# Seven block products in place of eight for half of the second MLP weight, with weight sums made by adding DMAs

## The chip, the cores and the metric

One Trainium2 chip, one of its cores. The metric is the device time of one execution in microseconds; less is better. Before the change it was 2324.06 us (median of three runs, 2323.91 to 2324.21).

## What is computed

Two layers over 256 tokens of width 2048, all in float32. Each layer is a mixer (a gated linear recurrence in layer 0, gated linear attention in layer 1) and then a dense squared-ReLU MLP; each of the four has a norm ahead of it and behind it and is added to the residual. The change concerns the MLP alone:

```python
def sqrelu_mlp(h, w_up, w_down):
    u = jax.nn.relu(h @ w_up)      # (256, 2048) @ (2048, 8192)
    return (u * u) @ w_down        # (256, 8192) @ (8192, 2048)

for i in range(DEPTH):
    ...
    f = sqrelu_mlp(rmsnorm(h, norm_mlp_pre[i]), mlp_w_up[i], mlp_w_down[i])
    h = h + rmsnorm(f, norm_mlp_post[i])
```

## The kernel before

Every matrix product runs on TensorE with both factors split in two parts: `hi`, the value rounded to the short form that TensorE multiplies in one pass, and `lo`, the rest. One product is then three matmuls, x_hi·w_hi, x_hi·w_lo and x_lo·w_hi (lines 122 to 127). A weight is read from HBM in chunks of 1 MB (`load_chunk`, line 96, always on SyncE's queue, three buffers `raw`), each of two halves of 128x1024. ScalarE makes `hi` of a half (line 102) and VectorE makes `lo` (line 106); five buffers of each are there, so at most five halves are split ahead of TensorE.

The MLP (`mlp`, line 475) goes through the 8192 hidden features in eight groups of 1024 (`GK` = 8 tiles of 128). `up(g)` computes one group of hidden features, transposed, eight times `gemmT` (16 matmuls of 512 columns with `hi`, 16 of 256 columns with `lo`), folds the two halves of the result, applies the squared ReLU and leaves the hi and lo parts in `uT[g]`. `down(g)` multiplies that group by its 1024 rows of `w_dn`: for each of four blocks of 512 output columns (`n`) it reads two chunks and runs `gemm` for both blocks of 128 tokens (`t`), 48 matmuls in all, then adds the two results onto the sums `m[n, t]` on VectorE (line 517). The order is up(0), up(1), down(0), up(2), down(1) and so on; the last block of columns of the last group is handed to `transition` or `final`, which finish the norm and start the next stage.

The code gives the order of the calls; the order in which each engine then gets its instructions is made by a scheduler that simulates the program, except inside blocks that fix it by hand (the start of the program and `transition`). Each engine and each queue works through its own instructions in that order. `Next` takes the first weight halves of the stage that follows ahead of time, into tiles that are free by then.

Of the kernel before, what the change touches and what calls it, by code (L numbers as in the profile page):

```python
# [18 lines left out]
P = 128  # L19
# [11 lines left out]
def trunk(  # L31
# [13 lines left out]
    halfp = ctx.enter_context(tc.tile_pool(name="half", bufs=6))  # L45
    featp = ctx.enter_context(tc.tile_pool(name="feat", bufs=1))
    accp = ctx.enter_context(tc.tile_pool(name="acc", bufs=1))
    small = ctx.enter_context(tc.tile_pool(name="small", bufs=4))
    psmm = ctx.enter_context(tc.tile_pool(name="psmm", bufs=4, space=PSUM))
    pssc = ctx.enter_context(tc.tile_pool(name="pssc", bufs=2, space=PSUM))  # L50
# [87 lines left out]
    def gemmT(wap, idx, X, pool=psmm, tag="mm"):  # L138


        ps = pool.tile([P, 2, T], F32, tag=tag, name=nm("mmT"))
        halves = split_chunk(wap, idx)
        for k in range(KT):
            hi = halves[k // 8][0][:, k % 8 * P:(k % 8 + 1) * P]
            PE.matmul(ps, hi, X.both(k), start=(k == 0), stop=False)  # L145
        for k in range(KT):
            lo = halves[k // 8][1][:, k % 8 * P:(k % 8 + 1) * P]
            PE.matmul(ps[:, 0, :], lo, X.both(k)[:, 0, :], start=False, stop=(k == KT - 1))  # L148
        return ps

    def fold(ps, rr=None):

        u = half()
        A.copy(u, ps[:, 1, :])  # L154
        V.tensor_tensor(u, ps[:, 0, :], u, ALU.add)  # L155
# [141 lines left out]
    def rrow(rs):  # L297
        ps = pstr.tile([P, NT, P], F32, tag="tr", name=nm("psr"))
        for t in range(NT):
            PE.matmul(ps[:, t, :], bc(rs[t], [P, P]), ident, start=True, stop=True)  # L300
        rr = small.tile([P, T], F32, tag="rr", bufs=1, name=nm("rr"))
        A.copy(rr, ps.rearrange("p a b -> p (a b)"))
        return rr

    class Post:
# [13 lines left out]
        def take(self, ps, n, t):  # L319
            self.square(ps, n, t)  # L320
            self.weigh(ps, n, t)
# [19 lines left out]
    class Next:  # L341

        def __init__(self, w, base):
            self.w, self.base, self.raws, self.parts, self.room = w, base, [], [], self.rooms()

        def rooms(self):
            def take(pool, tag, shape):
                return pool.tile(shape, F32R, tag=tag, name=nm(f"s{tag}"))  # L350

            qk = take(featp, "qk", [P, 2, 1024])
# [3 lines left out]
            b = take(big, "big", [P, 4, 1024])  # L356
            for j in range(2):
                yield b[:, 2 * j, :], b[:, 2 * j + 1, :]
            while True:
                yield None  # L360

# [112 lines left out]

    def mlp(layer, w_up, w_dn, X, rs, ps0, then=None):
        GK = 8
        NG = FF // (GK * P)
        uT = [None] * NG
        m = {}
        post = Post(2 + layer)  # L480

        rr = []

        def up(g):
            U = Xhl(GK)
            uT[g] = U
            for b in range(0, GK, 4):
                if g == 0 and b == 0:
                    for t in range(NT):
                        s = tok()  # L490
                        A.activation(s, ps0[t], AF.Relu, scale=rs[t])
                        A.activation(s, s, AF.Square)
                        put_split(transpose4(lambda j: s[:, j * P:(j + 1) * P]), U, 0, t)
                    rr.append(rrow(rs))
                    continue
                for j in range(b, b + 4):
                    u = fold(gemmT(w_up, g * GK + j, X))
                    V.scalar_tensor_tensor(u, u, 0.0, rr[0], ALU.max, ALU.mult)  # L498
                    hi, lo = U.both(j)[:, 0, :], U.both(j)[:, 1, :]
                    A.activation(hi, u, AF.Square)  # L500
                    A.activation(u, u, AF.Square)  # L501
                    V.tensor_tensor(lo, u, hi.bitcast(F32), ALU.subtract)  # L502

        ahead = Next(*then[1:]) if then is not None else None
        plan = {(NG - 2, 2): 2, (NG - 1, 0): 1, (NG - 1, 1): 1, (NG - 1, 2): 1}

        def down(g):
            for n in range(4 if g < NG - 1 else 3):
                ps = gemm(w_dn, n * 16 + 2 * g, GK, uT[g])
                if ahead is not None:  # L510
                    ahead.split(plan.get((g, n), 0))
                for t in range(NT):
                    if g == 0:
                        m[n, t] = tok()
                        V.tensor_copy(m[n, t], ps[t])
                        continue
                    V.tensor_tensor(m[n, t], m[n, t], ps[t], ALU.add)  # L517
                    if g == NG - 1:
                        post.take(m[n, t], n, t)

        up(0)
        for g in range(1, NG):
            up(g)
            down(g - 1)
        post.wp(3)
        down(NG - 1)
        args = (w_dn, 3 * 16 + 2 * (NG - 1), GK, uT[NG - 1], post, {t: m[3, t] for t in range(NT)})
        if then is not None:
            return transition(*args, then[0], ahead)
        final(*args)  # L530
# [412 lines left out]
```

## Time and profile before

| | |
|---|---|
| median of the runs | 2324.06 us |
| the profiled execution | 2323.86 us |
| its span, first to last instruction | 2322.1 us |
| TensorE busy | 2306.9 us, 99% |
| VectorE busy | 1505.1 us, 65% |
| ScalarE busy | 1217.5 us, 52% |
| bytes moved by DMA | 433.61 MB, 187 GB/s in the mean |

In the profile a line such as "PE ... L125" is a matmul that line 125 of the kernel issued; PEld is the load of its stationary operand, DVE is VectorE, ACT is ScalarE, POOL is GpSimd and SP is SyncE, which only issues DMAs here. Matmuls overlap in the pipeline, so what one costs is read from the distance between starts and not from its own duration.

### The profile page before, as it was taken

What the parts mean: (1) busy time and instruction counts of PE and PEld (TensorE: products, weight loads), DVE (VectorE), ACT (ScalarE), POOL (GpSimd) and SP (SyncE); (2) the same over time, 40 slices, a digit from 0 to 9 for tenths busy, and PEclk for the clock granted to TensorE, in tenths of its full rate; (3) what the DMA queues carried; (4) which work ended last, traced back from release to release, by engine and by line L of the source; (5) the groups of instructions that cost most, each with busy time, mean ns of one, the idle gap of its engine ahead of it and who ended that gap; (6) DMA issues with size and microseconds to landing.
All of it is one profiled execution on the core that took longest, in us unless ns stands there. A gap on an engine that the chain in (4) does not pass through costs nothing.

```text
span 2322.1 us, 29521 instructions
## 1 busy us (share of the span) xinstructions
PE 2306.9 (99%) x11720; PEld 1963.4 (85%) x11720; DVE 1505.1 (65%) x2111; ACT 1217.5 (52%) x1755; POOL 0.2 (0%) x4
## 2 busy tenths in 40 slices
PE   9999999999999999999999999999999999999998
PEld 7888888888888888888888888888888888888887
DVE  6887877656565565565676767566656556556556
ACT  7555554556454454454557456554645445445443
POOL 0000000000000000000000000000000000000000
PEclk9999999999999999999999999999999999999999
DMA  8544445545555555555654544454455555555553
GB/s 324 178 167 163 167 163 180 197 166 183 202 187 193 194 188 190 192 196 184 220 177 154 202 157 160 164 214 183 166 197 191 194 194 187 191 191 197 182 199 136
DMA packets 66155, 433.61 MB, mean 187 GB/s; under 512 B 8000, under 2 KB 8384, under 8 KB 15712
## 3 DMA queue, kind: packets, MB, share of 16 engines
q1 hardware_dynamic: 65872, 431.45, 53.8%
q8 instruction: 92, 1.51, 0.3%
q14 instruction: 47, 0.39, 0.0%
q10 hardware_dynamic: 144, 0.26, 0.0%
HBM read 429.59 MB, written 2.10 MB: 186 GB/s over the span
## 4 chain that ended last, share of the span: by engine, by line
PE 97%; DVE 2%; ACT 1%; issue 0%; DMA 0%; SPq 0%; DVEq 0%; ACTq 0%
PE mmT L145 27%; PE mm L127 18%; PE mm L126 18%; PE mm L125 18%; PE mmT L148 14%; PE sc L587 2%; DVE lo L106 1%; PE tr L181 1%; DVE xhl L194 0%; PE sd L622 0%; PE po L671 0%; PE po L674 0%; PE po L673 0%; ACT xhl L192 0%; DMA raw<-w_hin 0%
## 5 line engine op out<-in xcount | busy, mean ns | idle before, releaser
L106 DVE TENSOR_TENSOR lo<-raw,hi 128x1024 fp32r<-128x1024 f32 x779 | 939.2, 1223 | 523.1 <-ACT hi L102 394.2
L102 ACT ACTIVATE hi<-raw 128x1024 fp32r<-128x1024 f32 x779 | 823.3, 1061 | 777.6 <-PE mm L127 517.6
L125 PE MATMUL mm<-hi,xhl 128*128 128x512 f32 (+1 forms) x1804 | 704.3, 391 | 1.2 <-ACT hi L261 0.6
L126 PE MATMUL mm<-lo,xhl 128*128 128x512 f32 (+1 forms) x1804 | 702.7, 390 | 0.8 <-DVE lo L262 0.8
L127 PE MATMUL mm<-hi,xhl 128*128 128x512 f32 (+1 forms) x1804 | 701.7, 389 | 0.0
L145 PE MATMUL mmT<-xhl,hi 128*128 128x512 f32 x2704 | 655.4, 392 | 0.0
L145 PEld LDWEIGHTS mmT<-xhl,hi 128*128 128x128 f32 x2704 | 496.9, 188 | 97.4 <-issue 1.4
L125 PEld LDWEIGHTS mm<-hi,xhl 128*128 128x128 f32 x1804 | 339.2, 188 | 71.4 <-ACT hi L261 1.6
L126 PEld LDWEIGHTS mm<-lo,xhl 128*128 128x128 f32 x1804 | 339.3, 188 | 69.9 <-DVE lo L262 1.5
L127 PEld LDWEIGHTS mm<-hi,xhl 128*128 128x128 f32 x1804 | 339.2, 188 | 69.9 <-issue 0.6
L148 PEld LDWEIGHTS mmT<-xhl,lo 128*128 128x128 f32 x2704 | 347.3, 191 | 13.5 <-issue 0.5
L148 PE MATMUL mmT<-xhl,lo 128*128 128x256 f32 x2704 | 353.5, 283 | 0.0
L502 DVE TENSOR_TENSOR xhl<-half,xhl 128x256 fp32r<-128x256 f32 x120 | 50.7, 424 | 147.5 <-ACT half L501 147.5
L154 ACT COPY half<-mmT 128x256 f32<-128x256 f32 x169 | 62.7, 371 | 121.8 <-PE mmT L148 121.7
L155 DVE TENSOR_TENSOR half<-mmT,half 128x256 f32<-128x256 f32 x169 | 70.3, 417 | 0.6 <-ACT half L154 0.6
L517 DVE TENSOR_TENSOR tok<-tok,mm 128x512 f32<-128x512 f32 x108 | 69.0, 680 | 0.0
L500 ACT ACTIVATE xhl<-half 128x256 fp32r<-128x256 f32 x120 | 48.1, 402 | 26.3 <-DVE half L498 26.3
L498 DVE SCALAR_TENSOR_TENSOR half<-half,rr 128x256 f32<-128x256 f32 x120 | 50.8, 425 | 3.9
L501 ACT ACTIVATE half<-half 128x256 f32<-128x256 f32 x120 | 49.6, 415 | 3.2
L651 DVE TENSOR_TENSOR qk<-qk,tt 128x256 f32<-128x256 f32 (+1 forms) x96 | 46.6, 517 | 3.3 <-ACT kc L605 3.2
L192 ACT ACTIVATE xhl<-tr,prew 128x128 fp32r<-128x128 f32 x96 | 27.1, 374 | 34.0 <-PE tr L181 34.0
L194 DVE SCALAR_TENSOR_TENSOR xhl<-tr,prew,xhl 128x128 fp32r<-128x128 f32 x96 | 27.0, 344 | 21.6 <-ACT xhl L192 21.6
(167 smaller groups left out, 891.6 us busy)
## 6 DMA issues: line engine op xcount, KB each, us to landing
raw<-w_up SPq DMA_DIRECT2D x128, 1024.0 KB, 4.8
raw<-w_dn SPq DMA_DIRECT2D x128, 1024.0 KB, 4.8
raw<-w_hin SPq DMA_DIRECT2D x56, 1024.0 KB, 4.8
raw<-w_gin SPq DMA_DIRECT2D x48, 1024.0 KB, 4.8
raw<-w_hout SPq DMA_DIRECT2D x16, 1024.0 KB, 4.8
raw<-w_gout SPq DMA_DIRECT2D x16, 1024.0 KB, 5.0
raw<-w_hin SPq DMA_DIRECT2D x15, 512.0 KB, 6.8
wp<-npost SPq DMA_DIRECT2D x12, 256.0 KB, 4.2
```

Of the source, the lines that this page charges most:

```text
L102: A.activation(hi, raw, AF.Copy)
L106: V.tensor_tensor(half[1], raw, half[0].bitcast(F32), ALU.subtract)
L125: PE.matmul(ps, xh, hi[:, kk, cs], start=(k == 0), stop=False)
L126: PE.matmul(ps, xh, lo[:, kk, cs], start=False, stop=False)
L127: PE.matmul(ps, xl, hi[:, kk, cs], start=False, stop=(k == nk - 1))
L145: PE.matmul(ps, hi, X.both(k), start=(k == 0), stop=False)
L148: PE.matmul(ps[:, 0, :], lo, X.both(k)[:, 0, :], start=False, stop=(k == KT - 1))
L154: A.copy(u, ps[:, 1, :])
L155: V.tensor_tensor(u, ps[:, 0, :], u, ALU.add)
L498: V.scalar_tensor_tensor(u, u, 0.0, rr[0], ALU.max, ALU.mult)
L502: V.tensor_tensor(lo, u, hi.bitcast(F32), ALU.subtract)
L517: V.tensor_tensor(m[n, t], m[n, t], ps[t], ALU.add)
```

## The change

For the first 1024 output columns of `w_dn`, the two blocks n = 0 and n = 1, each group is treated as a product of matrices of two by two blocks: two blocks of tokens and two halves of the group's hidden features (512 each) on one side, those two halves and two blocks of 512 columns on the other. Done block by block that is eight products of 12 matmuls. The change does it in seven (`seven`), as Strassen's method in Winograd's form does: some products take sums of blocks in place of blocks.

- The sums on the side of the hidden features are made on the engines in `up` (`combine`): for each pair of feature tiles four VectorE operations of 128x128, one ScalarE copy and one VectorE subtraction of 128x512, 32 pairs in each MLP. They are kept, split in hi and lo, in tiles named `as`.
- The sums on the side of the weight are made by DMA. `begin_run` loads block (0, 0) into the tile `run` on SyncE's queue and adds block (0, 1) to it with an adding DMA on GpSimd's queue; after the product that reads `run`, block (1, 1) is added, after the next one block (1, 0). Three products of each group read `run`, with one adding DMA of 1 MB between one and the next. `begin_q` makes a second sum, of blocks (0, 1) and (1, 1), in two halves. Both belong to the next group as soon as the last reader of this group is through.
- The results of the seven products build up in three banks of PSUM, `sa`, `sb` and `sc`, and each product is added to or subtracted from one of the sums `m[n, t]` (`put`).
- The last 1024 columns (n = 2 and 3) stay as they were (`plain`, 48 matmuls each), but come a step later than the first: `down(g)` now runs the plain products of group g mixed with the seven products of group g + 1. The seven products of group 0 run by themselves, within up(1).
- `up` takes its tiles in the order 0, 4, 1, 5 and so on, `Next` has two more places, and the scratch for GpSimd's DMAs is halved.

```diff
+        def combine(to, a11, a12, a21, a22):
+            raw = tok().rearrange("p (a n) -> p a n", a=4)
+            s, r, s5, s3 = (raw[:, c, :] for c in range(4))
+            V.tensor_tensor(s, a11, a12, ALU.subtract)
+            V.tensor_tensor(r, a21, a11, ALU.subtract)
+            V.tensor_tensor(s5, s, a21, ALU.subtract)
+            V.tensor_tensor(s3, s5, a22, ALU.add)
+            A.activation(to[:, 0], raw, AF.Copy)
+            V.tensor_tensor(to[:, 1], raw, to[:, 0].bitcast(F32), ALU.subtract)
...
+        def add_to(raw, b):
+            nc.gpsimd.dma_start(raw, b, accum_op=ALU.add)
+
+        def begin_run(g):
+
+            raw = sump.tile([P, 2, 1024], F32, tag="run", name=nm("bs"))
+            nc.sync.dma_start(raw, block(g, 0, 0))
+            add_to(raw, block(g, 0, 1))
...
+        def begin_q(g):
+
+            sums["Q"] = [accp.tile([P, 1024], F32, tag=tag, name=nm("bs")) for tag in ("accA", "accB")]
+            for j in range(2):
+                nc.sync.dma_start(sums["Q"][j], block(g, 0, 1)[:, j, :])
+                add_to(sums["Q"][j], block(g, 1, 1)[:, j, :])
...
+            run = sums["run"], sums["tile"]
+            product("b", summed(0), run[0], 1, 0)
+            add_to(run[1], block(g, 1, 1))
+            product("a", pure(1, 0), raw_of(0, 0), 0, 1)
+            yield
+            product("c", pure(1, 1), raw_of(1, 0), 0, 1)
+            product("b", summed(3), raw_of(1, 1), 1, 1)
+            product("a", summed(2), run[0], 1, 1, -1)
+            add_to(run[1], block(g, 1, 0))
+            yield
+            product("a", summed(1), sums["Q"], 1, 0, -1)
+            if g < NG - 1:
+                begin_q(g + 1)
+            yield
+            product("a", pure(0, 1), run[0], 0, 0)
+            if g < NG - 1:
+                begin_run(g + 1)
...
         def down(g):
-            for n in range(4 if g < NG - 1 else 3):
-                ps = gemm(w_dn, n * 16 + 2 * g, GK, uT[g])
...
+            two, three, steps = plain(g, 2), plain(g, 3), seven(g + 1)
+            next(two)
+            next(two)
+            next(steps)
+            next(two, None)
+            next(steps)
+            next(three)
+            next(three)
+            next(steps)
+            next(three, None)
+            next(steps, None)
```

TensorE's rows in the down stage before, where one block of columns of the fifth group of MLP 0 is under way. `mm_7354` and `mm_7355` are its two blocks of tokens, `hi_7358` and `lo_7359` one half of a chunk, `xhl` the hidden features.

```order
L125 MATMUL mm_7354<-hi_7358,xhl_6192 128x512
L126 MATMUL mm_7354<-lo_7359,xhl_6192 128x512
L127 MATMUL mm_7354<-hi_7358,xhl_6192 128x512
...
L125 MATMUL mm_7355<-hi_7358,xhl_6192 128x512
```

The same engine in a down stage of MLP 0 of the change. `sb_7724` and `sa_7749` are banks of the seven products; `hi_7735` is the second half of `run` at its first use, `hi_7854` the first half of `run` at its second use, after one adding DMA; `mm_7688` is a plain product.

```order
L607 MATMUL sb_7724<-hi_7735,as_7308 128x512
L607 MATMUL sb_7724<-lo_7736,as_7308 128x512
...
L607 MATMUL sa_7749<-hi_7750,xhl_7256 128x512
...
L126 MATMUL mm_7688<-hi_7773,xhl_6513 128x512
...
L607 MATMUL sc_7809<-hi_7810,xhl_7256 128x512
...
L607 MATMUL sb_7724<-hi_7833,as_7307 128x512
...
L607 MATMUL sa_7749<-hi_7854,as_7307 128x512
```

A half that gave 12 matmuls to two banks gives six to one bank in the seven products. From the first matmul with `hi_7735` to the first with `hi_7854` stand 61 matmuls, all of 512 columns, 24 of them plain and the rest of the seven; from the second half of that second use to the third use stand 66 and then five of the next up stage.

The first group of an MLP has no plain products to mix with. These rows of TensorE are the ones between the first and the second use of `run` in the second MLP; `hi_14223` is the second half at the first use, `hi_14309` the first half at the second.

```order
L607 MATMUL sb_14212<-hi_14223,as_13981 128x512
L607 MATMUL sb_14212<-lo_14224,as_13981 128x512
...
L607 MATMUL sb_14212<-hi_14223,as_13982 128x512
...
L607 MATMUL sb_14212<-hi_14287,as_13980 128x512
...
L607 MATMUL sb_14212<-hi_14297,as_13982 128x512
L607 MATMUL sa_14238<-hi_14309,as_13980 128x512
```

Here 18 matmuls stand between, where a later group has 61.

SyncE's queue before, at the passage from a down stage to the next up stage.

```order
L96 DMA raw_7500<-w_dn 128x2048
L96 DMA raw_7534<-w_dn 128x2048
L96 DMA raw_7572<-w_up 128x2048
L96 DMA raw_7622<-w_up 128x2048
```

The same queue in the change. `bs_7933` and `bs_7934` are the two halves of the second sum, `bs_7996` is the tile `run`, each with its first block.

```order
L97 DMA raw_7939<-w_dn 128x2048
L97 DMA raw_8001<-w_up 128x2048
L97 DMA raw_8054<-w_up 128x2048
L572 DMA bs_7933<-w_dn 128x1024
L572 DMA bs_7934<-w_dn 128x1024
L97 DMA raw_8111<-w_up 128x2048
L563 DMA bs_7996<-w_dn 128x2048
L97 DMA raw_8161<-w_up 128x2048
```

The first blocks of the sums stand among the loads of the next up stage; seven chunks of `w_dn` are loaded in a group in place of eight. GpSimd's queue, which held no DMA before, holds five in each group: two of 512 KB and three of 1 MB.

More of the change, by code (lines that the diff above doesn't have):

```diff
@@ L355, in rooms @@
             yield take(accp, "accA", [P, 1024]), take(accp, "accB", [P, 1024])
-            b = take(big, "big", [P, 4, 1024])
-            for j in range(2):
-                yield b[:, 2 * j, :], b[:, 2 * j + 1, :]
+            run = take(sump, "run", [P, 2, 1024])
+            yield run[:, 0, :], run[:, 1, :]
+            if not big_first:
+                yield from in_big()
             while True:
@@ L486, in up @@
             uT[g] = U
-            for b in range(0, GK, 4):
-                if g == 0 and b == 0:
-                    for t in range(NT):
[L490 to L502, printed above, removed]
@@ L504, in mlp @@
-        ahead = Next(*then[1:]) if then is not None else None
-        plan = {(NG - 2, 2): 2, (NG - 1, 0): 1, (NG - 1, 1): 1, (NG - 1, 2): 1}
-        def down(g):
-            for n in range(4 if g < NG - 1 else 3):
-                ps = gemm(w_dn, n * 16 + 2 * g, GK, uT[g])
[L510 to L524, printed above, removed]
+            a = {}
+            js = [j + h for j in range(HK) for h in (0, HK)]
+            if g == 0:
+                for t in range(NT):
+                    s = tok()
+                    A.activation(s, ps0[t], AF.Relu, scale=rs[t])
+                    A.activation(s, s, AF.Square)
+                    ps = transpose4(lambda j: s[:, j * P:(j + 1) * P])
+                    put_split(ps, U, 0, t)
+                    raw = tok().rearrange("p (a n) -> p a n", a=4)
+                    A.copy(raw, ps)
+                    for j in range(HK):
+                        a[j, t] = raw[:, j, :]
+                rr.append(rrow(rs))
+                js = range(HK, GK)
@@ new lines, in up @@
+            for j in js:
+                u = fold(gemmT(w_up, g * GK + j, X))
+                V.scalar_tensor_tensor(u, u, 0.0, rr[0], ALU.max, ALU.mult)
+                hi, lo = U.both(j)[:, 0, :], U.both(j)[:, 1, :]
+                A.activation(hi, u, AF.Square)
+                A.activation(u, u, AF.Square)
+                V.tensor_tensor(lo, u, hi.bitcast(F32), ALU.subtract)
+                for t in range(NT):
+                    a[j, t] = u[:, t * P:(t + 1) * P]
+                if j == js[0]:
+                    yield
+                    sa[g] = sums_of_a(g)
+                if j >= HK:
+                    i = j - HK
+                    combine(sa[g][i], a[i, 0], a[j, 0], a[i, 1], a[j, 1])
@@ new lines, in block @@
+        def block(g, h, n):
+            return w_dn[n * 16 + 2 * g + h].rearrange("p (k n) -> p k n", k=2)
+        sums = {}
+        def add_to(raw, b):
[4 more added lines that the diff above has]
+            add_to(raw, block(g, 0, 1))
+            sums["run"] = [raw[:, j, :] for j in range(2)]
+            sums["tile"] = raw
@@ new lines, in mlp, with plain @@
+        ahead = Next(*then[1:], big_first=True) if then is not None else None
+        def plain(g, n):
+            ps = [psmm.tile([P, NB], F32, tag="mm", name=nm("mm")) for _ in range(NT)]
+            for c in range(2):
+                yield
+                for j, half in enumerate(split_chunk(w_dn, n * 16 + 2 * g + c)):
+                    for t in range(NT):
+                        mm_half(ps[t], half, 2 * c + j, uT[g], t, GK)
+            for t in range(NT):
+                put(n, t, ps[t])
@@ new lines, in down, with rest @@
+        def down(g):
+            two, three, steps = plain(g, 2), plain(g, 3), seven(g + 1)
[9 more added lines that the diff above has]
+            next(steps, None)
+        def rest(it):
+            for _ in it:
+                pass
+        for g in range(NG):
+            it = up(g)
+            next(it)
+            if g == 0:
+                begin_run(0)
+                begin_q(0)
+            if g == 1:
+                rest(seven(0))
+            rest(it)
+            if g:
+                down(g - 1)
@@ L525, in mlp @@
+        g = NG - 1
+        for n in range(2):
+            for t in range(NT):
+                post.take(m[n, t], n, t)
+        if ahead is not None:
+            ahead.split(2)
+        rest(plain(g, 2))
+        if ahead is not None:
+            ahead.split(3)
         post.wp(3)
-        down(NG - 1)
-        args = (w_dn, 3 * 16 + 2 * (NG - 1), GK, uT[NG - 1], post, {t: m[3, t] for t in range(NT)})
+        for t in range(NT):
+            post.take(m[2, t], 2, t)
+        args = (w_dn, 3 * 16 + 2 * g, GK, uT[g], post, {t: m[3, t] for t in range(NT)})
```

52 lines of the change are left out of this document (48 added, 4 removed).

## The prediction

> **What bounds the kernel now.** I read the first page first: span, busy times, the slices and the chain of work that ended last.
>
> ```profile
> span 2322.1 us, 29521 instructions
> PE 2306.9 (99%) x11720; PEld 1963.4 (85%) x11720; DVE 1505.1 (65%) x2111; ACT 1217.5 (52%) x1755; POOL 0.2 (0%) x4
> ...
> PE 97%; DVE 2%; ACT 1%; issue 0%; DMA 0%; SPq 0%; DVEq 0%; ACTq 0%
> ```
>
> TensorE is busy 99% of the span and carries 97% of the chain, so a matmul less is time less, as long as nothing else takes the gap. Next the windows, two in the middle of MLP 0 and the last one (columns: busy of PE, PEld, DVE, ACT, POOL with counts; granted clock, DMA share, GB/s).
>
> ```profile
> 700.00:800.00 100.00, 100.00 (x502) 85.28 (x502) 59.60 (x72) 47.99 (x61) 0.00 (x0) 1.00 0.56 191
> 800.00:900.00 100.00, 100.00 (x503) 85.28 (x502) 59.79 (x71) 47.27 (x62) 0.00 (x0) 1.00 0.56 192
> ...
> 2200.00:2322.00 122.00, 114.31 (x565) 97.00 (x563) 73.47 (x94) 51.64 (x74) 0.00 (x0) 0.98 0.49 168
> ```
>
> In the MLP TensorE never rests and the clock is full. VectorE is at 60%, the DMA engines at 56% with 191 GB/s; full they would move 191 / 0.56 = 341 GB/s, so a chunk of 1 MB (1.049 MB) takes all sixteen for 3.07 us. Last, TensorE's timeline over one group: the first row starts its up stage, the second its down stage, the third the next up stage.
>
> ```profile
> 721.59 3.79 PE L145 MATMUL mmT<-xhl,hi 128*128 128x512 f32 x16
> ...
> 766.10 0.40 PE L125 MATMUL mm<-hi,xhl 128*128 128x512 f32 x1
> 809.64 3.79 PE L145 MATMUL mmT<-xhl,hi 128*128 128x512 f32 x16
> ```
>
> Up takes 44.5 us. Down takes 43.54 us for 192 matmuls, 0.2268 us each. A group is 88.05 us.
>
> **What is removed.** Per group 12 of 192 down matmuls; the form (128x512, a stationary load each) stays. Eight groups in two MLPs: 192 x 0.2268 = 43.5 us off the path. A group becomes 44.5 + 180 x 0.2268 = 85.3 us. Everything below asks whether the other engines keep that pace.
>
> **VectorE and ScalarE.** These are the prices, from the groups by shape. The last three rows stand in for new shapes: L744 for a 128x128 sum, L617 for the 128x512 subtraction, L616 for its copy.
>
> ```profile
> L106 DVE TENSOR_TENSOR lo<-raw,hi 128x1024 fp32r<-128x1024 f32 x779 | 939.2, 1223 | 523.1 <-ACT hi L102 394.2 <-PE mmT L148 119.8 <-issue 7.6
> L155 DVE TENSOR_TENSOR half<-mmT,half 128x256 f32<-128x256 f32 x169 | 70.3, 417 | 0.6 <-ACT half L154 0.6
> L517 DVE TENSOR_TENSOR tok<-tok,mm 128x512 f32<-128x512 f32 x108 | 69.0, 680 | 0.0
> L498 DVE SCALAR_TENSOR_TENSOR half<-half,rr 128x256 f32<-128x256 f32 x120 | 50.8, 425 | 3.9
> L502 DVE TENSOR_TENSOR xhl<-half,xhl 128x256 fp32r<-128x256 f32 x120 | 50.7, 424 | 147.5 <-ACT half L501 147.5
> L102 ACT ACTIVATE hi<-raw 128x1024 fp32r<-128x1024 f32 x779 | 823.3, 1061 | 777.6 <-PE mm L127 517.6 <-PE mmT L145 212.1 <-DVE half L155 20.5
> L744 DVE TENSOR_TENSOR qk<-half,half 128x128 f32<-128x128 f32 x16 | 4.6, 289 | 4.9 <-ACT half L743 2.8 <-PE sc L587 2.0
> L617 DVE TENSOR_TENSOR dot<-tok,dot 128x512 fp32r<-128x512 f32 x18 | 12.4, 687 | 0.0
> L616 ACT ACTIVATE dot<-tok 128x512 fp32r<-128x512 f32 x18 | 11.3, 626 | 10.0 <-DVE tok L614 9.9
> ```
>
> Down, per group: 8 plain halves and 14 halves of the seven are 22 x 1.223 = 26.9 us, 11 additions to the sums (4 plain, 7) are 11 x 0.680 = 7.5: 34.4 us of VectorE in 40.8 (before: 16 halves and 8 additions, 25.0 in 43.5). Up: 16 x 1.223 + 8 x (0.417 + 0.425 + 0.424) = 29.7, and four pairs of sums at 4 x 0.289 + 0.687 = 1.84 add 7.4: 37.1 in 44.5. So VectorE goes to 84% in both stages. ScalarE has 22 x 1.061 = 23.3 us in the down stage and is not near. In the mean all of it hides.
>
> Within the down stage one place is tighter. A product of the seven takes TensorE 12 x 0.2268 = 2.72 us and VectorE 2 x 1.223 + 0.680 = 3.13; three stand in a row (sc, sb, sa), so VectorE falls 1.2 us behind. A plain chunk (5.44 us of TensorE, 2.45 of VectorE) gives that back on either side, but five buffers hold at most five halves of lead. Bounds: nothing, if the lead covers it, or 1.2 us in each of 16 groups, 19 us. I take 0.25 us a group, 4 us in all, near the lower end, since the trace shows VectorE idle for 523 us in front of L106 today, most of it only because it was ahead.
>
> **The adding DMAs.** The trace has none. The nearest row is the plain load of the same size:
>
> ```profile
> raw<-w_dn SPq DMA_DIRECT2D x128, 1024.0 KB, 4.8
> ```
>
> An addition has to fetch the new block and the tile that it adds to, and write back. Bounds: as quick as one load, 4.8 us to landing and 3.07 us of the engines; at the other end as costly as three loads in a row of the engines, 4.8 + 2 x 3.07 = 10.9 us and 9.2 us of the engines. I take two fetches: 7.9 us and 6.1 us.
>
> Engine load per group: 8 chunks of `w_up`, 7 of `w_dn` and 2 MB of first blocks are 17 x 3.07 = 52.2 us; four MB of additions bring 12.3, 24.6 or 36.8 us; in sum 64.5, 76.8 or 89.0 us in a group of 85.3 us. At the value taken it fits, at 90%; today it is 16 x 3.07 = 49 of 88.
>
> A page speaks to this: the Trainium skill, "Collectives: The Full Stack", section "The bandwidth ceiling: the fold count and why AG ≠ RS ≠ AR", says that a summing transfer runs at half the rate of a copy because it reads two sources, while the addition itself is free. By that rule the engine load is 76.8 us a group and the time is that of this forecast; by the upper bound of the rows it would be the slower rival below. No trace here shows it yet.
>
> Waiting: the next reader of `run` needs the addition landed, then ScalarE's 1.06 us and about 0.2 us of hand-over. The order puts 61 matmuls, 13.8 us, between first and second use in groups 1 to 7, and 66 and five, 16.1 us, between second and third. 7.9 + 1.3 = 9.2 us fits both, so does 10.9 + 1.3 = 12.2; even a landing at 14.4 us, three whole loads after each other, would cost 14 x 1.9 = 27 us. I take nothing. In the first group of each MLP there is less cover: by the same count 6.6 us (first MLP) and 18 matmuls, 4.1 us (second), then 10.5 us in both. Waits there: 9.2 - 6.6 = 2.6 and 9.2 - 4.1 = 5.1, nothing at 10.5: 7.7, say 8 us. With 4.8 us to landing it is 2 us, with 10.9 it is 5.6 + 8.1 + 2 x 1.7 = 17 us.
>
> **Queues.** While SyncE waits for the last reader of `run` or of the second sum, the loads of the next up stage behind it wait too. They are the third and fourth chunk of that stage, two chunks stand ahead, and the up stage needs one in 5.56 us: nothing. GpSimd had no work (0.2 us busy). The first additions for the next group have an up stage of 44.5 us. The four extra ScalarE copies per run of `up(0)` and the new order of tiles in `up` lie beside matmuls: nothing.
>
> **The sum.** 2323.9 (the profiled execution, 1.8 us over its span) - 43.5 + 8 + 4 = 2292.4 us. The profiled execution stands 0.2 us under the median, so 2292 holds for the runs too. About 0.2%, some 5 us, is what a measurement of this kernel tells from no change.
>
> **The rivals.**
>
> A. The adding DMAs fill the DMA engines, and the kernel is slower. One group then lasts as long as its transfers. The point from which it decides: 52.2 + 4X passes 85.3 us at X = 8.3 us per MB added, and eats the whole gain at 88 us, X = 9.0, close to the upper bound of 9.2. There: 16 x (89.0 - 85.3) = 59 us lost, and 17 us in the first groups: 2323.9 - 43.5 + 59 + 17 = 2356 us. For it: nothing here shows an adding DMA, and all other engines are idle for it. Against it: two fetches come out at 6.1. Waits would then also come in pieces longer than any today. The Trainium skill, "TensorE: Matmul & The Clock Gate", Part 1, adds that an idle window of about 3.4 us halves TensorE's clock; the windows before show 1.00, so no run here shows it, and by an estimate from that page one such window a group would add 16 x 1.7 = 27 us to this rival, 2383 us.
>
> B. VectorE becomes the bound in the down stage: 84% in the mean leaves little for its waits, for it stands idle behind ScalarE today in each `gemmT` (147.5 us before L502, 1.2 us each) and works strictly in order. If the 1.2 us of the three products stand in each of 16 groups and the sums of the up stage add 0.6 us in each group: 2292.4 - 4 + 29 = 2317 us, still faster.
>
> C. Nothing waits: 2323.9 - 43.5 = 2280 us, or 2282 with the quickest additions. That is the lower end of my own case.
>
> That seven products come out as fewer matmuls is certain from the order: 2880 in place of 3072.
>
> **How the numbers follow.** My case with C, 2280 to 2305 us: 0.55. B, 2305 to 2319: 0.17. About no change: 0.06. A, 2329 and above: 0.22; its price grows by 16 x 4 = 64 us for each microsecond per MB, so its tail is long. Faster 0.72, same 0.06, slower 0.22. The range leaves out the worst of A: 2278 to 2345 us. The likeliest case's own range is 2280 to 2305.
>
> **What would show it.** Right: about 192 fewer matmuls, TensorE over 98% busy in the windows of both MLPs, groups of 85 to 86 us, VectorE at about 80% there, DMA share near 0.9, waits of the matmuls for `run` only in the first group of each MLP. Wrong: landings of GpSimd's DMAs over 13 us, ScalarE's line 103 waiting for `bs` in every group (A), or matmuls waiting for `lo` in every group (B).

## The result and the profile after

The changed kernel takes 2309.4 us (median of 4 runs, 2308.8 to 2313.1) against 2324.0 (4 runs, 2323.7 to 2324.2) on the same chip: a ratio of 0.9941, 95% interval 0.9923 to 0.9958. It gains 14.6 us where the sum of the prediction said 31.5 (43.5 - 8 - 4). The profiled execution took 2309.34 us, its span is 2307.6 us, so 16.9 us are missing against the 2292.4 of the sum.

First the page of the changed kernel: span and busy times, the two DMA queues (packets, MB, share of 16 engines' span), the chain by engine, and the adding DMA of 1 MB with its median time from issue to landing.

```profile
span 2307.6 us, 30177 instructions
PE 2274.4 (99%) x11528; PEld 1931.4 (84%) x11528; DVE 1720.1 (75%) x2575; ACT 1328.5 (58%) x1919; POOL 69.4 (3%) x84
...
q1 hardware_dynamic: 70480, 448.23, 53.7%
q0 software_dynamic: 11520, 67.11, 15.4%
...
PE 94%; DVE 3%; DMA 1%; ACT 1%; issue 1%; SPq 0%; DVEq 0%; ACTq 0%
...
bs<-w_dn POOLq DMA_DIRECT2D x48, 1024.0 KB, 8.7
```

There are 11528 matmuls, 192 fewer than before. TensorE's share of the chain fell from 97% to 94%, so something else now stands on 6% of it in place of 3%. Where that is, the windows of the changed kernel say (columns: busy of PE, PEld, DVE, ACT and POOL with counts, then granted clock, DMA share, GB/s).

```profile
500.00:600.00 100.00, 91.17 (x438) 74.53 (x437) 67.83 (x115) 58.93 (x107) 7.04 (x8) 0.93 0.78 227
...
700.00:800.00 100.00, 100.00 (x517) 85.95 (x516) 77.33 (x113) 57.81 (x80) 5.17 (x6) 1.00 0.80 245
800.00:900.00 100.00, 100.00 (x503) 85.30 (x502) 79.30 (x110) 59.02 (x76) 4.31 (x5) 1.00 0.84 264
...
1600.00:1700.00 100.00, 91.43 (x452) 76.03 (x451) 69.19 (x122) 59.72 (x111) 6.91 (x8) 0.95 0.77 226
```

And the same two stretches of the kernel before:

```profile
500.00:600.00 100.00, 99.07 (x541) 85.53 (x540) 63.50 (x102) 61.73 (x116) 0.00 (x0) 1.00 0.49 169
1600.00:1700.00 100.00, 99.09 (x548) 85.60 (x547) 65.33 (x113) 62.51 (x125) 0.00 (x0) 1.00 0.43 148
```

Inside the MLPs TensorE is busy 100.00 of 100 us at full clock, with VectorE at 77 to 79% and the DMA engines at 0.80 to 0.84 in these two windows (75 to 80% and 0.80 to 0.85 in all full windows from 600 to 1100 and from 1700 to 2200): nothing is lost there. Where an MLP starts, 500 to 600 and 1600 to 1700, TensorE is busy 91% in place of 99%, and the clock in the mean 0.93 and 0.95. The pace of the steady groups is read from GpSimd's timeline: the first adding DMA inside `seven` comes once a group.

```profile
624.95 0.86 POOL L558 DMA_DIRECT2D bs<-w_dn  x1 [35.44 <-DVE tok L508]
...
710.28 0.86 POOL L558 DMA_DIRECT2D bs<-w_dn  x1 [41.56 <-DVE tok L508]
...
1136.94 0.86 POOL L558 DMA_DIRECT2D bs<-w_dn  x1 [40.75 <-DVE tok L508]
```

From the first to the last are six groups, 511.99 us, 85.33 each: the 85.3 of the prediction. So the loss is not in the steady groups; most of it is at the start of the MLPs. These are all of TensorE's waits in the changed kernel from 480 to 650 us (total us, times, longest).

```profile
PE sb L607 <- ACT as L511: 2.3, 1, 2.3
PE mm L128 <- DVE xhl L195: 2.1, 1, 2.1
PE sb L607 <- DVE as L512: 1.3, 1, 1.3
PE mmT L146 <- ACT hi L103: 1.1, 1, 1.1
PE sb L607 <- DVE tok L578: 0.8, 1, 0.8
PE sc L607 <- DVE lo L107: 0.6, 1, 0.6
PE sa L607 <- DVE lo L107: 0.5, 1, 0.5
```

Six of the seven stand in the first group: 6.6 us. In the second MLP the four waits of the first group are 2.3, 1.8, 1.7 and 0.8 us, again 6.6. One wait of 2.1 us stands in the transition from the output projection into the MLP, where the kernel before waits 0.93. TensorE's timeline shows what comes with the waits in the first group.

```profile
563.42 0.39 PE L607 MATMUL sc<-hi,xhl 128*128 128x512 f32 x1
566.06 0.80 PE L607 MATMUL sb<-hi,as 128*128 128x512 f32 x1 [2.26 <-ACT as L511]
...
568.61 0.80 PE L607 MATMUL sb<-hi,as 128*128 128x512 f32 x1 [1.32 <-DVE as L512]
570.19 0.80 PE L607 MATMUL sb<-hi,as 128*128 128x512 f32 x1 [0.78 <-DVE tok L578]
```

The same matmul takes 0.39 us in the first row and 0.80 us in the others: the clock is at half. The trace's clock records have four such pieces in the body of the run, one at each group of waits: 3.41 us (transition) and 10.24 us (first group) in the first MLP, 3.41 and 6.83 us in the second; before there was none. What that costs is, as an estimate, half of the time in which TensorE was busy there. The windows view over just these four stretches of the changed kernel sums to:

```profile
sum 23.90, PE 18.55 PEld 13.48 DVE 17.82 ACT 4.93 POOL 1.72; mean PE 4.64 PEld 3.37 DVE 4.45 ACT 1.23 POOL 0.43
```

So 18.55 / 2 = 9.3 us: 1.7 at each transition, 3.5 and 2.3 in the two first groups (7.08 and 4.63 us busy).

The account: first groups 2 x 6.6 us of waits and 5.8 of clock, 19.0; transitions into the MLPs 2 x 1.14 (2.07 against 0.93, 2.05 against 0.91) and 3.4 of clock, 5.7; the transition behind the first MLP 2.7 us of waits (2.3 and 0.4) against 1.6, 1.1; the first 500 us, which the change doesn't touch, 0.8 more idle time. Together 26.6 us of the 29.0 between 43.5 and the 14.5 us gained by the profiled execution; 2.4 are not assigned. The whole span says nearly the same: TensorE's idle time grew from 15.2 to 33.2 us, and these 18 with the 9.3 of clock are 27.3. (The expectations below take the half clock at half of its whole length, 5.1 and 3.4 us in the first groups, and so call them 21.7 us.)

### The profile page after: what moved, and what is told of

Read it like the earlier page. It is cut to its first block, busy times and chain, and to the rows that moved or that the text cites. A ratio compares the mean times of both kernels' runs of the same rounds, so it can differ in the third digit from the quotient of the medians.

```text
span 2307.6 us, 30177 instructions
## 1 busy us (share of the span) xinstructions
PE 2274.4 (99%) x11528; PEld 1931.4 (84%) x11528; DVE 1720.1 (75%) x2575; ACT 1328.5 (58%) x1919; POOL 69.4 (3%) x84
## 3 DMA queue, kind: packets, MB, share of 16 engines
q1 hardware_dynamic: 70480, 448.23, 53.7%
q0 software_dynamic: 11520, 67.11, 15.4%
## 4 chain that ended last, share of the span: by engine, by line
PE 94%; DVE 3%; DMA 1%; ACT 1%; issue 1%; SPq 0%; DVEq 0%; ACTq 0%
PE mmT L146 26%; PE mmT L149 14%; PE mm L128 13%; PE mm L127 13%; PE mm L126 13%; PE sa L607 7%; PE sb L607 4%; PE sc L607 2%; PE sc L743 2%; DVE lo L107 1%; DMA bs<-w_dn 1%; PE tr L182 1%; DVE xhl L195 0%; PE sd L778 0%; DMA raw<-w_hin 0%
## 5 line engine op out<-in xcount | busy, mean ns | idle before, releaser
L127 PE MATMUL mm<-lo,xhl 128*128 128x512 f32 (+1 forms) x1280 | 498.3, 389 | 1.3 <-DVE lo L263 1.2
L128 PE MATMUL mm<-hi,xhl 128*128 128x512 f32 x1280 | 496.9, 389 | 0.0
L126 PE MATMUL mm<-hi,xhl 128*128 128x512 f32 x1280 | 487.4, 391 | 1.4 <-ACT hi L262 0.8
L126 PEld LDWEIGHTS mm<-hi,xhl 128*128 128x128 f32 x1280 | 240.6, 188 | 51.7 <-ACT hi L262 2.4
L127 PEld LDWEIGHTS mm<-lo,xhl 128*128 128x128 f32 x1280 | 240.5, 188 | 50.7 <-DVE lo L263 2.7
L128 PEld LDWEIGHTS mm<-hi,xhl 128*128 128x128 f32 x1280 | 240.4, 188 | 49.2 <-issue 0.2
L103 ACT ACTIVATE hi<-bs 128x1024 fp32r<-128x1024 f32 x128 | 135.3, 1059 | 95.2 <-PE mm L128 37.8
L107 DVE TENSOR_TENSOR lo<-bs,hi 128x1024 fp32r<-128x1024 f32 x128 | 153.8, 1221 | 37.4 <-ACT hi L103 33.9
L558 POOL DMA_DIRECT2D bs<-w_dn x80 | 69.2, 865 | 2188.0 <-DMA bs<-w_dn 1186.8
L607 PE MATMUL sb<-hi,as 128*128 128x512 f32 x256 | 91.3, 408 | 9.4 <-ACT as L511 4.5
L607 PE MATMUL sa<-hi,xhl 128*128 128x512 f32 x256 | 84.2, 389 | 0.0
L607 PE MATMUL sa<-hi,as 128*128 128x512 f32 x256 | 84.0, 389 | 0.0
L155 ACT COPY half<-mmT 128x256 f32<-128x256 f32 x169 | 60.8, 360 | 33.3 <-PE mmT L149 33.2
```

The source lines that it names most:

```text
L103: A.activation(hi, raw, AF.Copy)
L107: V.tensor_tensor(half[1], raw, half[0].bitcast(F32), ALU.subtract)
L126: PE.matmul(ps, xh, hi[:, kk, cs], start=(k == 0), stop=False)
L127: PE.matmul(ps, xh, lo[:, kk, cs], start=False, stop=False)
L128: PE.matmul(ps, xl, hi[:, kk, cs], start=False, stop=(k == nk - 1))
L558: nc.gpsimd.dma_start(raw, b, accum_op=ALU.add)
```

## The experiments

Three theories went in. **D** is the step on record: the first group waits for the adding DMAs into `run`. **V**: it waits for VectorE, which has to make the sums of hidden features (`as`) beside the splits. For V speaks that VectorE's timeline has no idle time between these two rows of the changed kernel, 545.39 and 567.88, and that the second makes the last `as`:

```profile
540.87 1.23 DVE L107 TENSOR_TENSOR lo<-raw,hi 128x1024 fp32r<-128x1024 f32 x1 [4.12 <-ACT hi L103]
...
545.39 0.69 DVE L190 TENSOR_TENSOR xhl<-tr,xhl 128x512 fp32r<-128x512 f32 x1 [2.96 <-ACT xhl L189]
...
567.88 0.68 DVE L512 TENSOR_TENSOR as<-tok,as 128x512 fp32r<-128x512 f32 x1
```

For D speaks that VectorE had idled 4.12 and 2.96 us just before. **R** concerns the transitions: the read-ahead class `Next` got one more room, `run`.

All kernels that keep the whole computation and all that leave some out are in one table; "before" ran on the same chip in each batch, at 2323.7 to 2324.0 us. The runs of one of these kernels lie up to 6 us apart, so a difference of one or two microseconds between two rows is not told from none by the medians; where the text leans on such a difference, it goes by the waits in the traces.

| kernel | median us | runs from, to | ratio to before, 95% |
|---|---|---|---|
| changed kernel | 2309.4 | 2308.8, 2313.1 | 0.9941 (0.9923, 0.9958) |
| no_adds_g0 | 2304.4 | 2303.3, 2305.6 | 0.9917 (0.9903, 0.9930) |
| no_sums_g0 | 2308.0 | 2307.2, 2311.1 | 0.9936 (0.9924, 0.9949) |
| no_adds_no_sums_g0 | 2290.6 | 2289.9, 2291.0 | 0.9855 (0.9841, 0.9870) |
| hold3 | 2308.8 | 2305.5, 2311.9 | 0.9935 (0.9923, 0.9948) |
| spread0 | 2293.8 | 2291.7, 2295.2 | 0.9869 (0.9854, 0.9883) |
| block_g0 | 2291.4 | 2289.4, 2294.4 | 0.9860 (0.9845, 0.9875) |
| no_run_room | 2313.4 | 2312.3, 2316.8 | 0.9958 (0.9946, 0.9971) |
| room_big_only | 2307.4 | 2305.8, 2309.4 | 0.9927 (0.9911, 0.9944) |
| plain_dma | 2304.8 | 2303.8, 2306.3 | 0.9918 (0.9905, 0.9932) |
| double_adds | 2556.6 | one run | |
| block_g0_room | 2286.9 | 2286.7, 2287.0 | 0.9841 (0.9827, 0.9854) |
| spread0_room | 2295.6 | 2293.9, 2297.5 | 0.9879 (0.9865, 0.9892) |

**The adding DMAs of the first group left out (no_adds_g0).**

```
+        def add_later(g, raw, b):
+            if g:
+                add_to(raw, b)
...
-            add_to(raw, block(g, 0, 1))
+            add_later(g, raw, block(g, 0, 1))
```

(the same at the other adds of `begin_q` and `seven`)

> The adding DMAs of the first group of each MLP are left out (five of them, 4 MB each time); the plain loads and all products stay, so the first group's share of the first 1024 columns is computed from the wrong weight sums. Theory V (VectorE: the changed kernel's waits at the start of each MLP come from the sums of hidden-feature blocks, which VectorE has to make beside the splits): nothing or little goes, 2306 to 2310 us against 2309.4. Theory D (my recorded step: those waits come from the adding DMAs into the first group's rooms, directly or because they hold up the w_up load that VectorE then waits 4.12 us for at 540 us): the waits of the first groups, 6.6 us in each MLP, and the half clock behind them, 5.1 and 3.4 us, go for the most part: 2289 to 2298 us.

Measured 2304.4: 1.6 us below V's span and 6 above D's. The waits on the sums stay, 2.0 + 1.0 + 0.8 us in the first MLP and 2.3 + 1.8 + 0.8 in the second. D as it stood falls: without any adding DMA there the first group still waits, and only 5.0 us of the 19.0 went.

**The sums of hidden features of the first group left out (no_sums_g0).**

```
-                    combine(sa[g][i], a[i, 0], a[j, 0], a[i, 1], a[j, 1])
+                    if g:
+                        combine(sa[g][i], a[i, 0], a[j, 0], a[i, 1], a[j, 1])
...
             def summed(c):
+                if g == 0:
+                    return pure(c % 2, c // 2)
```

> The sums of hidden-feature blocks of the first group alone are left out (20 VectorE and 4 ScalarE instructions in each MLP); its products take blocks of the plain hidden features instead, so its share of the first 1024 columns is wrong; all adding DMAs and all matmuls stay. Theory V: the waits on these sums (2.3 + 1.3 + 0.8 us in the first MLP) and the half clock after them go, 2290 to 2297 us. Theory D: the adding DMAs still come as late, so at most the part that V calls direct goes, 2303 to 2308 us.

Measured 2308.0, the upper edge of what D said: V falls too, at least as the one cause. TensorE's waits of this kernel from 480 to 660 us show why:

```profile
PE mmT L146 <- ACT hi L103: 5.6, 1, 5.6
PE sa L611 <- DVE tok L582: 2.7, 1, 2.7
PE mm L128 <- DVE xhl L195: 2.0, 1, 2.0
PE sc L611 <- DVE lo L107: 0.2, 1, 0.2
```

The waits on `as` are gone, and the last one of the first group, for ScalarE's split, has grown from 1.1 to 5.6 us. (The 2.7 us are for VectorE's addition that frees the bank `sa`; in VectorE's order it stands behind four splits of `bs`.) The origin of the 5.6 us is read from three engines, GpSimd, ScalarE and TensorE, in this kernel:

```profile
566.30 0.86 POOL L560 DMA_DIRECT2D bs<-w_dn  x1 [12.79 <-DVE lo L107]
```
```profile
577.55 2.00 ACT L103 ACTIVATE hi<-bs 128x1024 fp32r<-128x1024 f32 x2 [11.73 <-DMA bs<-w_dn]
```
```profile
580.55 5.54 PE L146 MATMUL mmT<-xhl,hi 128*128 128x512 f32 x16 [5.59 <-ACT hi L103]
```

This is the adding DMA between the second and the third use of `run`. It is issued at 566.30, and the split that reads its result can begin only 11.2 us later; ScalarE stands 11.73 us before that split, and behind it in ScalarE's order stand those of `w_up`, for which TensorE waits. In the second MLP the same takes 10.4 us, from 1668.56 to 1678.95, and TensorE waits 6.0. It is D's chain. In the changed kernel it is there too and nearly hidden, by the waits on the sums ahead of it. So a new theory, **S** (series): two chains stand behind one another in the first group, and whichever is taken away uncovers the other.

**More transposed products ahead of the first group's seven (hold3).** This belongs with those two, before S; `last` is `js[2]` for the second group and `js[0]` for the others.

```
-                if j == js[0]:
+                if j >= HK:
+                    pending.append(j)
+                if j == last:
                     yield
                     sa[g] = sums_of_a(g)
```

> The first group's seven products start after three transposed products of the second group in place of one; all 84 products, sums and adding DMAs stay. Theory V: VectorE gets two more transposed products of 5.57 us each, of which it needs some 75 per cent for their own splits, so 2.8 us of slack against waits of 4.4 us; with the last wait under a microsecond the clock stays whole: 2290 to 2299 us. Theory D, if the adding DMAs are merely late by some microseconds: the same 11 us cover them too, 2289 to 2295 us; if adding DMAs cost through the whole group, no change, 2307 to 2311 us. This run says whether the loss sits at the start of the MLPs at all; the two runs beside it say which work makes it.

Measured 2308.8, no change: neither V's range nor D's first one, and the number of D's last case, in which adding DMAs cost through the whole group. The traces don't show that case. TensorE's waits from 480 to 660 us:

```profile
PE mmT L146 <- ACT hi L103: 5.2, 1, 5.2
PE sa L613 <- DVE tok L586: 2.7, 1, 2.7
PE mm L128 <- DVE xhl L195: 2.1, 1, 2.1
```

It is the picture of no_sums_g0: the sums now come in time, and the chain on `run`, which can only go on when the first of the seven products has split its weights, is as long as before and stands against 84 matmuls in one block, 84 x 0.2268 = 19 us.

**Both left out (no_adds_no_sums_g0):** the two edits above together.

> Both things are left out in the first group of each MLP, its adding DMAs and its sums of hidden features (its share of the first 1024 columns is wrong twice over; all matmuls stay). Theory S (series: two chains stand one behind the other there, the sums on VectorE, then the adding DMAs into run one after another; each alone hides most of the other, which is why leaving out the adds brought 5.0 us and leaving out the sums 1.4): all waits of the first groups, 6.6 us in each MLP, and the half clock behind them, 5.1 and 3.4 us, go: 2288 to 2292 us. If the two gains merely add, 5.0 + 1.4, and something else holds the first group: 2301 to 2305 us.

Measured 2290.6, as S said: 18.8 us against the changed kernel, where the two alone brought 5.0 and 1.4. Of the waits of the first groups only 1.1 us is left in each MLP, for `w_up`'s split, and no half clock behind it. This shows that the two chains together are the loss of the first groups, and that what each brings alone does not add up.

**The same work in another order (spread0).** The four parts of `seven(0)` go between the transposed products of the second group.

```
-                if j == js[0]:
+                made += 1
...
+                if g == 1 and 2 <= made <= 5 or g != 1 and made == 1:
                     yield
...
             if g == 1:
-                rest(seven(0))
+                first = seven(0)
+                for _ in range(4):
+                    next(first, None)
+                    next(it, None)
```

> Nothing is left out: the first group's seven products are cut into their four parts, which stand between the second group's transposed products (after the second, third, fourth and fifth of them) in place of in one block behind the first. Theory S: the sums get one transposed product more (5.57 us) and each adding DMA into run 8 to 13 us of matmuls to land behind, against 11.2 us that it took: 2288 to 2297 us. If adding DMAs and w_up loads are simply too much for the DMA engines in this stretch, the waits move and stay: 2303 to 2311 us.

Measured 2293.8, with nothing left out: 15.6 us under the changed kernel. The waits left in the first groups are 1.9 us (first MLP) and 2.6 us (second).

**The first group by plain blocks (block_g0).**

```
             if g == 1:
-                rest(seven(0))
+                rest(plain(0, 0))
+                begin_run(1)
+                begin_q(1)
+                rest(plain(0, 1))
```

(`begin_run(0)`, `begin_q(0)` and the first group's sums of hidden features go too)

> The first group of each MLP is computed by plain blocks, 96 matmuls in place of 84 (12 more of 0.2268 us, 2.72 us in each MLP), without sums of hidden features and without adding DMAs of its own; the second group's adding DMAs start in the same place as its plain loads. Theory S: 21.7 us of waits and half clock go, 5.4 us come: 2293 to 2295 us. If the second group then takes over the first one's waits: 2305 to 2315 us.

Measured 2291.4, a little under the expectation. From 480 to 660 us TensorE has one wait left, the 2.1 us at the transition.

**The room (no_run_room, room_big_only).** In the first kernel the lines of `Next.rooms` that take `run` go, in the second they stand under `if big_first:`.

> The split weights that a transition reads ahead no longer use the room of the weight sums (run); the rest stays as in the changed kernel. Theory R (that room lets one more split onto VectorE and ScalarE ahead of the hidden-feature transposes of the transition; TensorE waits 2.07 and 2.05 us instead of 0.93 and 0.91 there, and its clock is halved for 3.41 us after each): 2 x (1.1 + 1.7) = 5.6 us go, and up to 0.7 at the transition behind the first MLP, 2303 to 2304 us. If the longer waits come from elsewhere (the first adding DMAs, or another order of the whole), nothing goes: 2308 to 2311 us.

> The split weights read ahead use the room of the weight sums (run) at the transition behind the first MLP only, no longer at those into the two MLPs. Theory R, as it stands after no_run_room (there TensorE's wait at the transitions into the MLPs fell to 0.9 us as foretold, but the transition behind the first MLP, which lost its room too, waited for w_gin's weights instead): 2 x (1.1 + 1.7) = 5.6 us go, and nothing is lost: 2302 to 2306 us. If the room's absence costs elsewhere, at the start of the MLPs: 2307 to 2313 us.

What R says of the transitions is in VectorE's and TensorE's timelines. Changed kernel:

```profile
505.28 4.63 DVE L107 TENSOR_TENSOR lo<-raw,hi 128x1024 fp32r<-128x1024 f32 x4
```
```profile
510.22 0.67 PE L128 MATMUL mm<-sqk,xhl 128*128 128x512 f32 x1 [2.07 <-DVE xhl L195]
```

Kernel before:

```profile
505.18 3.49 DVE L106 TENSOR_TENSOR lo<-raw,hi 128x1024 fp32r<-128x1024 f32 x3
```
```profile
508.99 0.50 PE L127 MATMUL mm<-sqk,xhl 128*128 128x512 f32 x1 [0.93 <-DVE xhl L194]
```

Four splits in place of three stand on VectorE ahead of the hidden-feature transposes; one is 1.15 us, and TensorE waits 1.14 us longer. With the room gone the wait is 0.9 us in both kernels, as foretold, and no half clock follows there. But no_run_room came out at 2313.4, 4.0 us slower than the changed kernel and not 5.6 faster, and room_big_only at 2307.4, 2.0 faster, which the scatter of the runs covers, and not 5.6. In the first the transition behind the first MLP lost its room too: TensorE was busy 97.35 us from 1100 to 1200, where the changed kernel has 100.00. In both, the first groups wait longer. Here room_big_only, from 480 to 660 us:

```profile
PE mmT L146 <- ACT hi L103: 2.9, 1, 2.9
PE sb L608 <- DVE as L513: 1.7, 2, 0.9
PE sb L608 <- ACT as L512: 1.7, 1, 1.7
PE sb L608 <- DVE tok L579: 1.2, 1, 1.2
PE mm L128 <- DVE xhl L195: 0.9, 1, 0.9
```

Its first groups wait 7.5 and 7.1 us, 1.4 more than 2 x 6.6, which takes back the larger part of the 2.3 us that the transitions saved; by the profiles, what is left of the gain is clock. The stretches of half clock of room_big_only sum to:

```profile
sum 17.01, PE 15.00 PEld 11.45 DVE 10.01 ACT 5.28 POOL 1.22; mean PE 5.00 PEld 3.82 DVE 3.34 ACT 1.76 POOL 0.41
```

That is 7.5 us lost in place of 9.3. So R is right about its place and its mechanism, and wrong about its worth as long as the first groups are late. The reason is open: that the split which is no longer made in the transition is then made in the first group, on the chain that is late there, fits this, but is argued and was not tried by itself.

**What an adding DMA costs (plain_dma, double_adds).**

```
-            nc.gpsimd.dma_start(raw, b, accum_op=ALU.add)
+            nc.gpsimd.dma_start(raw, b)
```

(in double_adds the line as it was, twice)

> Every adding DMA becomes a plain one of the same bytes on the same queue, so that the weight blocks are overwritten and not summed (the first 1024 columns are wrong); every instruction of the compute engines stays in its place. Theory of two fetches (as in my recorded working: an adding DMA reads what it adds to as well, and holds the DMA engines nearly twice as long; GpSimd's queue took 15.4% of 16 engines' span for 64 MB, 5.55 us per MB, the plain queue 53.7% for 427 MB, 2.90 us per MB): the queue's share falls to about 8%, and the landing from 8.7 us to 5 or 6. Rival (it is GpSimd's queue that is slow): the share stays near 15%. Time, by theory S: the steady groups hide it either way, and in the first group the sums on VectorE still come late: 2303 to 2309 us.

> Every adding DMA is issued twice (the weight sums are wrong), so that their load doubles: the DMA engines' share of 0.83 in the steady groups of 85.3 us is 70.8 us, and four more adds of 5.55 us make 93.0 us. Rival A of the prediction (adding DMAs fill the DMA engines) with the dose that it would need: at least 7.7 us more in each of 16 groups, 2430 us or above, since the chain on run gets longer as well (each second add lands behind the first, 17 us in place of 8.7). If there were far more room than the share says: under 2340 us.

Plain copies on the same queue, in the page of plain_dma:

```profile
q0 software_dynamic: 11520, 67.11, 8.3%
...
bs<-w_dn POOLq DMA_DIRECT2D x48, 1024.0 KB, 5.2
```

The queue's share is 8.3% in place of 15.4%, the landing 5.2 us in place of 8.7: the addition costs 1.86 times a copy, and the queue itself is not slow. The time is 2304.8, 4.6 us under the changed kernel, about as much as leaving the first group's adds out brought (5.0): TensorE is full in the steady groups with either kind, so what an adding DMA costs over a copy can show in the first groups alone. With every add issued twice the kernel takes 2556.6 us, 247 more. Windows and the largest wait for an added block in double_adds:

```profile
700.00:1000.00 300.00, 272.04 (x1328) 228.57 (x1329) 205.58 (x287) 150.82 (x205) 27.63 (x32) 0.95 0.93 269
```
```profile
ACT hi L103 <- DMA bs<-w_dn: 382.6, 35, 16.8
```

At twice the dose the picture of rival A appears, in the one run of this kernel: the DMA engines are at 0.93 and ScalarE's line 103 waits for `bs` through the whole MLP, 16.8 us at the longest. Load and the longer chain on `run` grew together here, so their parts of the 247 us are not told apart, and it isn't shown that full DMA engines alone would do it.

**Put together (block_g0_room, spread0_room).**

> The first group of each MLP by plain blocks, and the room of the weight sums used by read-ahead only behind the first MLP; the result is the reference's. Theories S and R: 2291.4 less 2 x 1.1 us of waits at the transitions into the MLPs, and less half clock there in those executions that have it (up to 1.7 us at each): 2286 to 2290 us. If the two edits undo each other: 2291 to 2295 us.

> The first group's products spread over the second group's transposed products, and the room of the weight sums used by read-ahead only behind the first MLP; all 84 products per group stay. Theories S and R: 2293.8 less 2 x 1.1 us of waits and less the half clock of some executions: 2288 to 2292 us, behind block_g0_room by the waits that spread0 kept (1.9 and 2.6 us) less the 5.4 us of matmuls that it saves. If the two edits undo each other: 2293 to 2298 us.

The first came out at 2286.9 us, the fastest of all: a ratio of 0.9841 (0.9827 to 0.9854) to the kernel before, 22.5 us under the changed kernel, with nothing of the computation left out. Its windows:

```profile
500.00:600.00 100.00, 99.09 (x523) 84.91 (x523) 64.11 (x106) 60.80 (x112) 1.73 (x2) 1.00 0.58 190
1600.00:1700.00 100.00, 100.00 (x535) 86.41 (x534) 63.01 (x103) 59.12 (x102) 1.73 (x2) 1.00 0.61 199
```

The start of the MLPs is as full as in the kernel before. The second, at 2295.6, missed: the transitions wait 0.9 us, but the first groups 5.6 and 3.9 us in place of 1.9 and 2.6, which looks like the exchange in room_big_only. Which of VectorE's instructions makes it is open.

## Why the prediction was right in part and wrong in size

**Right: what is removed, and the steady groups.** 192 matmuls fewer, 85.33 us a group against 85.3, VectorE at 75 to 80% where the list of signs said about 80%, DMA share 0.80 to 0.85 where 0.9 was said. The 43.5 us are there: a steady group takes 85.33 us in place of 88.05, 2.72 less, and 16 x 2.72 is 43.5.

**Right: two fetches.** The prediction took 6.1 us of the engines per MB and 7.9 us to landing. The queue's 15.4% of 2307.6 us over 64 MB is 5.55 us, the landing 8.7. The plain queue's 53.7% over 427 MB is 2.90 us per MB, so that a group's load is 17 x 2.90 + 4 x 5.55 = 71.5 us of 85.3, or 0.84, which is what the windows show. The trace agrees with the rule cited from the Trainium skill, "Collectives: The Full Stack", section "The bandwidth ceiling: the fold count and why AG ≠ RS ≠ AR", which states it for the reduce step of a ring: 1.86 times a copy here, a little under its factor of two. So rival A, which needed 8.3 us per MB, did not come, and took doubling all adds to show.

**Wrong by its whole size, but small: VectorE in the steady groups.** 4 us were put there; TensorE's 100.00 leaves nothing. The 84% of the working took each instruction at its own duration, but neighbours overlap: two splits in a row take 2.35 us (VectorE's row at 562.79), not 2 x 1.223. The measured time lies in the interval given to rival B, 2305 to 2319 us, but not on B's path, since no steady group waits for VectorE.

**The step that failed: the waits of the first groups.** The prediction counted one chain there, the additions into `run`, and got 8 us, all of it at the second use of `run`. Two things in this step were wrong.

It put the other chain at nothing: the sums of hidden features were priced in the mean, 37.1 us of VectorE in a stage of 44.5, and said to hide. In the first group they don't have that stage. Half of each pair comes through the transposes of the read-ahead columns, all four pairs fall due within four transposed products, and the splits of the seven products stand between them in VectorE's order. The waits are 13.2 us, not 8, and as the two chains stand in series, neither edit alone could bring them back.

It also had the place of its own chain wrong. With the sums out of the way (no_sums_g0) TensorE doesn't wait at the second use, where 2.6 and 5.1 us were forecast. It waits ahead of the third, where the prediction counted 10.5 us of cover against 9.2 and put nothing. From the issue of that adding DMA to the start of the split that reads it are 11.2 and 10.4 us, where 7.9 to landing were taken. And of the 10.5 us about 6.4 (by the changed kernel's rows) are matmuls of the up stage, whose own splits stand behind that of `run` in ScalarE's order: they are late with it and cover nothing. The chain costs 5.6 - 1.1 and 6.0 - 1.1 us of waits for ScalarE's split, 9.4 in all (1.1 is what is left without either chain). That this is near 8 is luck.

**The same step again: the clock.** It was counted in rival A only, for idle windows of about 3.4 us, as the Trainium skill, "TensorE: Matmul & The Clock Gate", Part 1, has them. The half clock came with waits of 2.3, 1.3 and 0.8 us close together, and behind a single wait of 2.07. In the first groups it added 5.8 us to 13.2 of waits. 19.0 in place of 8 is 11.0 of the 16.9 us by which the forecast was off.

**Not in the sum at all: the room.** One line of the diff gives the read-ahead a place more. The prediction read the new order of the groups and not that of the transitions: 5.7 us there and 1.1 behind the first MLP. With 0.8 in the first 500 us, and less the 4 us of VectorE that did not come, 11.0 + 6.8 + 0.8 - 4 = 14.6 of the 16.9 us are named.

## What to carry to other kernels

Price a new chain where it starts, not only where it is steady: in the first turn of a loop there is no earlier turn's work to hide behind, and 7 in 8 turns at full pace say nothing about it. Where two late things stand in series on one engine's path, take both away before judging either, and don't add up what each brings alone. If a faster scheme has a long start, the slower one for the first turn only can be cheaper (here 5.4 us of matmuls for 19.0 of waits and half clock), and an extra buffer for read-ahead can lengthen a wait when it lets work in ahead of what is waited for (here by 1.14 us).

## What the runs showed of the hardware that was not expected

- TensorE's clock goes to half behind waits well under 3.4 us. All pieces of half clock in the body of the traces are one to four times 3.413 us long. At the two transitions into the MLPs, in the nine profiles where the wait is 2.0 to 2.1 us, a piece of 3.41 us follows in 9 of 18 places, in the ten places (five profiles) where it is 0.9 us never. The Trainium skill, "TensorE: Matmul & The Clock Gate", Part 1, asks for an idle window of about 3.4 us; the length of the pieces agrees with it, the waits of 2 us that sufficed do not.
- Which of the 18 it is, the traces tell. The pieces of one trace all begin on one grid of 3.413 us, and the grid stands elsewhere in each execution. If the traces are cut along it, and a window's idle time is what the matmul rows leave of it, then in the fourteen profiles (without the first 30 us and the end) the clock halved behind each of the 55 windows of full clock with 1.9 us or more of idle time, behind two of the nine with 1.7 to 1.9, and behind none with less. All 57 pieces are among these. The first row here is the window ahead of the piece at the first transition in the changed kernel, TensorE busy for 1.34 us; the others are the two windows over which the same wait of 2.07 us falls in block_g0, which has no piece there.

```profile
506.98:510.39 3.41, 1.34 (x7) 0.78 (x6) 3.41 (x6) 0.62 (x3) 0.00 (x0) 1.00 0.75 269
```
```profile
505.94:509.35 3.41, 2.63 (x14) 1.85 (x12) 3.41 (x4) 2.09 (x9) 0.00 (x0) 1.00 0.40 96
509.35:512.76 3.41, 2.12 (x9) 1.77 (x10) 3.41 (x10) 0.00 (x0) 0.00 (x0) 1.00 1.02 418
```

- So a wait of 2 us brings half clock when it falls nearly whole into one window, and one of 0.9 us alone stays under what it takes. The runs of block_g0 lie 5 us apart (2289.4 to 2294.4), with a mean clock of 0.999 in the quickest and 0.997 in the slowest; those of block_g0_room, without that wait, 0.3 us apart (2286.7 to 2287.0), all at 0.999. That the clock makes the scatter fits this, but is not shown: block_g0_room keeps 2.3 us of wait behind the first MLP, which in two other profiles (no_adds_g0, no_sums_g0) came with half clock, and the runs of no_adds_no_sums_g0, with both waits of 2 us, lie only 1.1 us apart.
